# Decays of a gated recurrence from one running sum per 128 tokens, and state products that nobody reads left out

## The chip, the core and the metric

The kernel runs on one core of a Trainium2 chip. The metric is the device time of one launch in microseconds (us), as the median of several runs. The engines of the core are named as in the profile: PE is TensorE (PEld its weight loads), DVE is VectorE, ACT is ScalarE, POOL is GpSimd, SP is SyncE. All five have an instruction queue of their own and work through it in order.

## The reference, cut to what matters

The kernel is an encoder trunk of two layers over 1024 tokens of width 1024: layer 0 mixes tokens by windowed attention, layer 1 by a bidirectional gated linear recurrence, each with a cross attention into 256 memory tokens and each followed by a convolutional feed-forward block. The change lies in the recurrence of layer 1:

```python
def gla_chunked(q, k, v, log_f):          # called once forward, once on flipped time
    b = jnp.cumsum(log_f, axis=2)         # within a chunk
    b_end = b[:, :, -1:]
    q_dec = q * jnp.exp(b)
    k_dec = k * jnp.exp(-b)
    k_end = k * jnp.exp(b_end - b)
    s = jnp.where(causal, q_dec @ k_dec.T, 0)      # inside the chunk
    o_intra = s @ v
    # scan over chunks, per head:
    #   o     = q_dec @ state
    #   state = exp(b_end) * state + k_end.T @ v
```

There are 8 heads with 128 key and 128 value channels. The result does not depend on the size of the chunk, apart from rounding; the state after the last chunk is read by nothing.

## The kernel before

**Staging.** The program is one long stream in which PE has work nearly all the time. The parts follow one another: memory keys and values, layer 0's attention, its output projection, its feed-forward block, then `hgrn()` (layer 1's recurrence, about 1230 to 1910 us of the span), layer 1's output projection and its feed-forward block. Matrix products of weights are done in three products of split operands (`mm3`, lines 79 to 82: high by high, high by low, low by high).

**Order of the instructions.** The source gives a program order; a planner with estimated costs walks through it and sets the order of each engine's queue, taking what it believes to be ready. `tc.high_priority(AHEAD)` lets a group be taken as if it stood 2000 instructions earlier, `tc.issue_after(x)` holds a group until x. Waits for data and for free buffers are put in by the framework: a tile with `bufs=n` has n buffers, and the (n+1)th allocation waits until the readers of the first are done.

**A head.** `proj(h)` makes the projections of head h: q (`sigmoid` on ACT, lines 1091 to 1093, and a product on DVE, line 1129), the two gate inputs `s` (one exponential on ACT, line 1134), and for two heads at a time values and gates (`proj_tm`, lines 1095 to 1115). They land in two PSUM banks `pj`, which ACT and DVE must empty before PE can use them again. `head(h)` then calls `direction` four times, for (forward, tokens 0 to 511), (backward, 512 to 1023), (forward, 512 to 1023) and (backward, 0 to 511), then `output` for both halves. The projections of head h + 1 stand behind it in program order and fill PE while `direction` works on the other engines. `cross` adds the cross attention's pieces in heads 0, 2, 4 and 6; such a head reads its memory keys and values into `kvl` by a DMA, and ACT casts them (line 193).

**`direction`** has keys and channels on the 128 partitions and 512 tokens (four chunks of 128) on the free axis. Four ACT steps make k and the log gate `a_` (lines 1177 to 1180). A scan on DVE sums the log gate, restarted every 16 tokens by `smask`, into `B` (line 1182); `R` is the rest to the end of the 16 (line 1185). ACT makes `EP = exp(B)` and `ER = exp(R)`, and the reciprocals for one half of each pair of 16s (lines 1202, 1203). Four half-size products on DVE give `E1`, `E2`, the operands of the blocks of 32 by 32 tokens on the diagonal. `step(n)` then doubles the reach of EP and ER from n to 2n tokens by two half-size products on DVE (lines 1217, 1218); it is called for 16, 32 and 64. After the first two, `G` for 32 and for 64 is made by one half-size product on POOL (line 1225) and one on DVE (line 1226). 64 small products on PE (`block`, line 1210) fill `pa`, the matrix inside the chunk.

With the reach at 128, EP and ER serve the state: `dec` (POOL, line 1243) takes EP's last column per chunk, `qin` (POOL, line 1245) is EP times q, ER is multiplied by k (DVE, line 1246), turned by four transposes on PE into the bank `pt` (line 1256), copied by ACT to `kT` (line 1258), and multiplied by the values into the bank `pu` (line 1261), four products. The states `S` of the next chunks come from `pu` (lines 1268, 1270). For a chunk without a next one the loop skips the state, but its transpose and its product have been made. `pa` goes through a predicated copy (line 1247) into `Az` and `As`. `output` multiplies `As`, `qin` and `S` into the result, and writes heads 0 to 6 to memory by way of `ot` (line 1315).

A DMA on POOL's queue that sums weights for the feed-forward block in memory (`w2s`) is tied to each `qin` by `sum_steps`.

Of the kernel before, what the change touches and what calls it, by code (L numbers as in the profile page):

```python
# [46 lines left out]
def build(tc, A, out):  # L47
# [983 lines left out]
    def hgrn():  # L1031
# [130 lines left out]
        def direction(h, r, d, b, qin, S, As):  # L1162

            q, k = r["q"][b], r["s"][d][b]
            rev = slice(None, None, -1) if d else slice(None)
            lt, er = (0, 1) if d else (1, 0)

            def E():
                return early.tile([P, 512], F32, tag="E", bufs=5, name="E")
# [6 lines left out]
            a_ = E()  # L1176
            act.activation(k, k, AF.Ln, bias=1.0)
            act.activation(k, k, AF.Exp, scale=-1.0)
            act.activation(a_, k, AF.Ln, bias=lb[:, d, h:h + 1], scale=oml[:, d, h:h + 1])
            act.activation(k, k, AF.Identity, bias=oml[:, d, h:h + 1], scale=noml[:, d, h:h + 1])  # L1180
            R, B = E(), E()
            dve.tensor_tensor_scan(B[:, rev], smask, a_[:, rev], 0.0, op0=ALU.mult, op1=ALU.add)
            v16 = lambda x: x.rearrange("p (b c) -> p b c", c=16)
            e = 0 if d else 15
            dve.tensor_tensor(v16(R), bc(v16(B)[:, :, e:e + 1], [P, 32, 16]), v16(B), op=ALU.subtract)
# [3 lines left out]
            act.activation(EP, B, AF.Exp)  # L1189
            act.activation(ER, R, AF.Exp)  # L1190
            pa = PA[d]
            E1, E2 = E(), E()
            Bl, Be = halves(B, 16)
            Rl, Re = halves(R, 16)
            l1, e1 = halves(E1, 16)
            l2, e2 = halves(E2, 16)

            def parts(n):
                return halves(EP, n) + halves(ER, n) + halves(q, n) + halves(k, n)

            pl_, pe_, rl_, re_, ql, qe, kl, ke = parts(16)
            act.activation(e1, Re, AF.Exp, scale=-1.0)
            act.activation(l2, Bl, AF.Exp, scale=-1.0)
            dve.tensor_tensor(l1, pl_, ql, op=ALU.mult)
            dve.tensor_tensor(e2, re_, ke, op=ALU.mult)
            dve.tensor_tensor(e1, e1, qe, op=ALU.mult)
            dve.tensor_tensor(l2, l2, kl, op=ALU.mult)
            def block(c, i, j, x, y, n=32):

                return pe.matmul(pa[i:i + 32, c, j:j + n], x[:, c * P + i:c * P + i + 32], y[:, c * P + j:c * P + j + n],  # L1210
                                 start=True, stop=True, tile_position=(0, i))

            def step(n):
                pl_, pe_, rl_, re_ = parts(n)[:4]
                e = 0 if d else n - 1
                nb = 512 // (2 * n)
                dve.tensor_tensor(re_, re_, bc(pl_[:, :, e:e + 1], [P, nb, n]), op=ALU.mult)
                dve.tensor_tensor(pl_, pl_, bc(pe_[:, :, e:e + 1], [P, nb, n]), op=ALU.mult)

            for n in (32, 64):  # L1220
                step(n // 2)
                G = E()
                gl, ge = halves(G, n)
                pl_, pe_, rl_, re_, ql, qe, kl, ke = parts(n)
                pool.tensor_tensor(gl, pl_, ql, op=ALU.mult)
                dve.tensor_tensor(ge, re_, ke, op=ALU.mult)
                if n == 32:
                    G32 = G
            with tc.high_priority(AHEAD):
                for c in range(4):  # L1230
                    for o in (0, 32):
                        mm = block(c, er * 64 + o, lt * 64, G, G, 64)
                with tc.issue_after(mm.ins):
                    for c in range(4):
                        for o in range(0, P, 32):
                            block(c, o, o, E2, E1)
                    for c in range(4):
                        for o in (0, 64):
                            block(c, o + er * 32, o + lt * 32, G32, G32)
# [3 lines left out]
            pool.tensor_copy(dec.unsqueeze(2), EP.rearrange("p (c t) -> p c t", t=P)[:, :, e:e + 1])  # L1243
            bs = slice(b * 512, (b + 1) * 512)
            sum_steps[1].send(pool.tensor_tensor(qin[:, bs], EP, q, op=ALU.mult))
            dve.tensor_tensor(ER, ER, k, op=ALU.mult)
            dve.copy_predicated(Az[d], gm[d], pa.rearrange("p c t -> p (c t)"))
            a2 = lambda x: x.rearrange("p c t -> p (c t)")
            if As[b] is None:
                As[b] = wp.tile([P, 4, P], F32, tag="As", bufs=2, name="As")  # L1250
                act.copy(a2(As[b]), Az[d])
            else:
                pool.tensor_tensor(a2(As[b]), a2(As[b]), Az[d], op=ALU.add)
            tp = bank("pt")
            for c in range(4):
                pe.transpose(tp[:, c, :], ER[:, c * P:(c + 1) * P], ident)
            kT = wp.tile([P, 4, P], F32, tag="kT", bufs=1, name="kT")
            act.copy(kT, tp)
            pu = bank("pu")
            for c in range(4):  # L1260
                pe.matmul(pu[:, c, :], kT[:, c, :], r["v"][:, 4 * b + c, :], start=True, stop=True)
            for c in (range(3, -1, -1) if d else range(4)):
                cg = 4 * b + c
                nx = cg - 1 if d else cg + 1
                if not 0 <= nx < NT:
                    continue
                if cg == (NT - 1 if d else 0):
                    act.copy(S[:, nx, :], pu[:, c, :])
                else:
                    dve.scalar_tensor_tensor(S[:, nx, :], S[:, cg, :], dec[:, c:c + 1], pu[:, c, :],  # L1270
                                             op0=ALU.mult, op1=ALU.add)
# [300 lines left out]
```

## Time and profile before

| | us |
|---|---|
| median of 3 runs (lowest to highest) | 2664.08 (2660.1 to 2664.66) |
| time of the profiled execution | 2660.75 |
| its span, first to last instruction | 2658.9 |
| PE busy in it | 2605.2 |
| DVE busy | 1771.2 |
| ACT busy | 1399.1 |
| POOL busy | 472.2 |

The profiled execution is 1.85 us longer than its span, and lies 3.3 us under the median. Busy times are sums over the span; a pipelined matmul counts as busy until its end, so a busy PE isn't PE at its peak. An idle entry behind a row says how long the engine had nothing to do before these instructions, and whose work ended that.

### The profile page before, as it was taken

To read this page: it belongs to the slowest core of one execution; us is meant where nothing else is said; L and a number is where in the kernel's file an instruction comes from. 1 tells how busy PE (TensorE), PEld (TensorE's weight loads), DVE (VectorE), ACT (ScalarE), POOL (GpSimd) and SP (SyncE) were. 2 spreads that over 40 slices of the span, in tenths; PEclk is the share of its full clock that TensorE was granted. 3 is DMA by queue.
4 is the path that set the end of the run, shared out by engine and by line. 5 is a ranking of instruction groups with operands and counts; after the bars stand their busy time and mean duration, and the time that the engine had idled before them with its cause. 6 is when DMAs were issued, how large, how long until landed. Compare 5 with 4: busy or idle time off the path is not lost. (4 is left out here: it accounts for less than half of the span.)

```text
span 2658.9 us, 39054 instructions
## 1 busy us (share of the span) xinstructions
PE 2605.2 (98%) x14420; PEld 2185.9 (82%) x14420; DVE 1771.2 (67%) x2948; ACT 1399.1 (53%) x2534; POOL 472.2 (18%) x520
## 2 busy tenths in 40 slices
PE   8999999999999999999999999999999999999998
PEld 7888887788888888887888878888887788888887
DVE  6678886578555565477677675876757755656447
ACT  6467676545444445455464554656534444445453
POOL 0321010211111100032234131231211111110013
PEclk9999999999999999999999999999999999999999
DMA  9782222367777756674236251103336778785666
GB/s 353 243 176 58 74 86 83 101 193 194 198 201 195 206 154 221 215 265 151 84 112 167 66 124 54 53 25 113 127 105 195 194 193 209 198 202 170 205 207 236
DMA packets 195727, 425.92 MB, mean 160 GB/s; under 512 B 20048, under 2 KB 56272, under 8 KB 189904
## 3 DMA queue, kind: packets, MB, share of 16 engines
q1 hardware_dynamic: 161552, 324.06, 37.6%
q0 software_dynamic: 24544, 90.19, 16.3%
q10 hardware_dynamic: 9440, 9.19, 1.0%
q8 instruction: 113, 1.85, 0.3%
q14 instruction: 78, 0.64, 0.1%
HBM read 330.04 MB, written 116.39 MB: 168 GB/s over the span
## 5 line engine op out<-in xcount | busy, mean ns | idle before, releaser
L86 DVE TENSOR_TENSOR wl<-st,wh 128x1024 fp32r<-128x1024 f32 (+1 forms) x238 | 261.4, 1105 | 316.8 <-ACT wh L85 294.1
L85 ACT CAST wh<-st 128x1024 fp32r<-128x1024 f32 (+1 forms) x238 | 222.4, 937 | 288.7 <-PE X L574 186.5
L80 PE MATMUL pj<-uh,wh 128*128 128x512 f32 x512 | 203.6, 398 | 2.2 <-DVE q L1129 0.8
L574 PE MATMUL X<-wl,wh 128*128 128x512 f32 x528 | 205.0, 390 | 0.3 <-DVE wl L86 0.3
L574 PE MATMUL X<-wh,wl 128*128 128x512 f32 x528 | 204.9, 389 | 0.0
L81 PE MATMUL pj<-ul,wh 128*128 128x512 f32 x512 | 202.4, 395 | 0.0
L82 PE MATMUL pj<-uh,wl 128*128 128x512 f32 x512 | 202.3, 395 | 0.0
L574 PE MATMUL X<-wh 128*128 128x512 f32 x528 | 198.6, 390 | 0.0
L80 PE MATMUL pj<-wh,uh 128*128 128x384 f32 (+1 forms) x512 | 189.4, 372 | 5.0 <-DVE gs L1115 2.6
L82 PE MATMUL pj<-wh,ul 128*128 128x384 f32 (+1 forms) x512 | 187.7, 367 | 0.0
L81 PE MATMUL pj<-wl,uh 128*128 128x384 f32 (+1 forms) x512 | 187.2, 366 | 0.0
L76 DVE TENSOR_TENSOR wl<-st,wh 128x1024 fp32r<-128x1024 f32 (+1 forms) x91 | 113.9, 1256 | 30.9 <-ACT wh L75 29.8
L574 PE MATMUL V<-uh,wh 128*128 128x512 f32 x336 | 130.7, 389 | 0.0
L574 PE MATMUL V<-ul,wh 128*128 128x512 f32 x336 | 130.7, 389 | 0.0
L574 PE MATMUL V<-uh,wl 128*128 128x512 f32 x336 | 130.7, 389 | 0.0
L75 ACT CAST wh<-st 128x1024 fp32r<-128x1024 f32 (+1 forms) x97 | 97.8, 1014 | 37.5 <-PE pj L81 16.4
L574 PEld LDWEIGHTS X<-wl,wh 128*128 128x128 f32 x528 | 99.1, 188 | 21.6 <-DVE wl L86 1.2
L574 PEld LDWEIGHTS X<-wh,wl 128*128 128x128 f32 x528 | 99.1, 188 | 20.7
L574 PEld LDWEIGHTS X<-wh 128*128 128x128 f32 x528 | 99.1, 188 | 20.5
L80 PEld LDWEIGHTS pj<-uh,wh 128*128 128x128 f32 x512 | 96.5, 189 | 21.7 <-DVE q L1129 1.2
L82 PEld LDWEIGHTS pj<-uh,wl 128*128 128x128 f32 x512 | 96.5, 189 | 19.0
L81 PEld LDWEIGHTS pj<-ul,wh 128*128 128x128 f32 x512 | 96.5, 188 | 18.6 <-DVE ul L86 0.4
(411 smaller groups left out, 7149.2 us busy)
## 6 DMA issues: line engine op xcount, KB each, us to landing
st<-hid SPq DMA_DIRECT2D x154, 256.0 KB, 3.4
st<-in_ffw_dram SPq DMA_DIRECT2D x108, 256.0 KB, 3.7
w2s<-in_ffw_dram POOLq DMA_DIRECT2D x24, 1024.0 KB, 8.0
st<-in_ffw_dram SPq DMA_DIRECT2D x46, 512.0 KB, 4.3
hid<-tt SPq DMA_DIRECT2D x88, 256.0 KB, 4.7
st<-w2s SPq DMA_DIRECT2D x88, 256.0 KB, 3.2
sx<-in_ffw_dram SPq DMA_DIRECT2D x84, 256.0 KB, 3.9
sy<-in_ffw_dram SPq DMA_DIRECT2D x42, 512.0 KB, 6.4
```

Of the source, the lines that this page charges most:

```text
L75: act.copy(h[:, :n], raw)
L76: (eng or dve).tensor_tensor(l[:, :n], raw, h[:, :n].bitcast(F32), op=ALU.subtract)
L80: pe.matmul(o, ah, bh, start=first, stop=False)
L81: pe.matmul(o, ah, bl, start=False, stop=False)
L82: return pe.matmul(o, al, bh, start=False, stop=last)
L85: act.copy(h, src)
L86: dve.tensor_tensor(l, src, h.bitcast(F32), op=ALU.subtract)
L574: last = pe.matmul(o, x, y, start=new, stop=e, skip_group_check=not first)
```

## The change

It is all in `hgrn()`. `smask` now restarts the scan every 128 tokens, so B is the sum over a whole chunk. For the reach 16, 32 and 64 a new function subtracts from B its value at the middle of each pair (one full-size subtraction on DVE), and ACT takes exponentials of that difference: two of full size for E1 and E2, two of half size for each G, which the products with q (POOL) and k (DVE) then change in place. `R`, the reciprocals and `step` are gone. EP is the exponential of B itself, ER one exponential per chunk with B's last column as bias, and both are made after the blocks in program order. For the chunk whose state is not read, ER's piece, the transpose and the product are left out, and the copies beside them are shorter. Buffers: tag E has 4 instead of 5, EP and ER 1 each instead of 2, and new tags D (2) and B (1) are added; the sum of buffers is 9 before and after.

```diff
-            gf = early.tile([P, 512], F32, tag="E", bufs=5, name="gf")
+            gf = early.tile([P, 512], F32, tag="E", bufs=4, name="gf")
...
-        pool.memset(smask.rearrange("p (b c) -> p b c", c=16)[:, :, 0:1], 0.0)
+        pool.memset(smask.rearrange("p (b c) -> p b c", c=P)[:, :, 0:1], 0.0)
...
-            R, B = E(), E()
+            B = E("B", 1)
             dve.tensor_tensor_scan(B[:, rev], smask, a_[:, rev], 0.0, op0=ALU.mult, op1=ALU.add)
-            dve.tensor_tensor(v16(R), bc(v16(B)[:, :, e:e + 1], [P, 32, 16]), v16(B), op=ALU.subtract)
-            EP = early.tile([P, 512], F32, tag="EP", bufs=2, name="EP")
-            ER = early.tile([P, 512], F32, tag="ER", bufs=2, name="ER")
-            act.activation(EP, B, AF.Exp)
-            act.activation(ER, R, AF.Exp)
+            def from_middle(n):
+                D = E("D", 2)
+                v = lambda x: x.rearrange("p (b c) -> p b c", c=2 * n)
+                m = n if d else n - 1
+                dve.tensor_tensor(v(D), v(B), bc(v(B)[:, :, m:m + 1], [P, 512 // (2 * n), 2 * n]), op=ALU.subtract)
+                return D
+            D = from_middle(16)
+            E1, E2 = E(), E()
+            act.activation(E1, D, AF.Exp)
+            act.activation(E2, D, AF.Exp, scale=-1.0)
+            dve.tensor_tensor(E1, E1, q, op=ALU.mult)
+            dve.tensor_tensor(E2, E2, k, op=ALU.mult)
...
-            act.activation(e1, Re, AF.Exp, scale=-1.0)
-            act.activation(l2, Bl, AF.Exp, scale=-1.0)
-            dve.tensor_tensor(l1, pl_, ql, op=ALU.mult)
-            dve.tensor_tensor(e2, re_, ke, op=ALU.mult)
-            dve.tensor_tensor(e1, e1, qe, op=ALU.mult)
-            dve.tensor_tensor(l2, l2, kl, op=ALU.mult)
...
             for n in (32, 64):
-                step(n // 2)
-                pool.tensor_tensor(gl, pl_, ql, op=ALU.mult)
-                dve.tensor_tensor(ge, re_, ke, op=ALU.mult)
+                D = from_middle(n)
+                G[n] = E()
+                act.activation(gl, dl, AF.Exp)
+                act.activation(ge, de, AF.Exp, scale=-1.0)
+                pool.tensor_tensor(gl, gl, ql, op=ALU.mult)
+                dve.tensor_tensor(ge, ge, ke, op=ALU.mult)
...
-            step(64)
+            used = [c for c in range(4) if 4 * b + c != (0 if d else NT - 1)]
+            EP, ER = E("EP", 1), E("ER", 1)
+            act.activation(EP, B, AF.Exp)
+            for c in used:
+                x = slice(c * P, (c + 1) * P)
+                m = c * P + (0 if d else P - 1)
+                act.activation(ER[:, x], B[:, x], AF.Exp, bias=B[:, m:m + 1], scale=-1.0)
...
-            dve.tensor_tensor(ER, ER, k, op=ALU.mult)
+            us_ = slice(used[0] * P, (used[-1] + 1) * P)
+            dve.tensor_tensor(ER[:, us_], ER[:, us_], k[:, us_], op=ALU.mult)
...
-            for c in range(4):
+            for c in used:
                 pe.transpose(tp[:, c, :], ER[:, c * P:(c + 1) * P], ident)
...
-            act.copy(kT, tp)
+            act.copy(kT[:, cs_], tp[:, cs_])
...
-            for c in range(4):
+            for c in used:
                 pe.matmul(pu[:, c, :], kT[:, c, :], r["v"][:, 4 * b + c, :], start=True, stop=True)
```

More of the change, by code (lines that the diff above doesn't have):

```diff
@@ L1166, in direction, with E @@
             lt, er = (0, 1) if d else (1, 0)
-            def E():
-                return early.tile([P, 512], F32, tag="E", bufs=5, name="E")
+            def E(tag="E", bufs=4):
+                return early.tile([P, 512], F32, tag=tag, bufs=bufs, name=tag)
             def halves(x, n):
@@ L1211, in block @@
                                  start=True, stop=True, tile_position=(0, i))
[L1213 to L1218, printed above, removed]
-            for n in (32, 64):
-                step(n // 2)
[L1222 to L1225, printed above, removed]
-                dve.tensor_tensor(ge, re_, ke, op=ALU.mult)
-                if n == 32:
-                    G32 = G
+            G = {}
+            for n in (32, 64):
+                D = from_middle(n)
+                G[n] = E()
+                (dl, de), (gl, ge), (ql, _), (_, ke) = (halves(x, n) for x in (D, G[n], q, k))
+                act.activation(gl, dl, AF.Exp)
+                act.activation(ge, de, AF.Exp, scale=-1.0)
+                pool.tensor_tensor(gl, gl, ql, op=ALU.mult)
+                dve.tensor_tensor(ge, ge, ke, op=ALU.mult)
             with tc.high_priority(AHEAD):
@@ L1231, in direction @@
                     for o in (0, 32):
-                        mm = block(c, er * 64 + o, lt * 64, G, G, 64)
+                        mm = block(c, er * 64 + o, lt * 64, G[64], G[64], 64)
                 with tc.issue_after(mm.ins):
@@ L1238, in direction @@
                         for o in (0, 64):
-                            block(c, o + er * 32, o + lt * 32, G32, G32)
-            step(64)
+                            block(c, o + er * 32, o + lt * 32, G[32], G[32])
+            used = [c for c in range(4) if 4 * b + c != (0 if d else NT - 1)]
[5 more added lines that the diff above has]
+                act.activation(ER[:, x], B[:, x], AF.Exp, bias=B[:, m:m + 1], scale=-1.0)
             dec = wp.tile([P, 4], F32, tag="dec", bufs=2, name="dec")
@@ L1254, in direction @@
             tp = bank("pt")
-            for c in range(4):
+            for c in used:
                 pe.transpose(tp[:, c, :], ER[:, c * P:(c + 1) * P], ident)
             kT = wp.tile([P, 4, P], F32, tag="kT", bufs=1, name="kT")
-            act.copy(kT, tp)
+            cs_ = slice(used[0], used[-1] + 1)
+            act.copy(kT[:, cs_], tp[:, cs_])
             pu = bank("pu")
-            for c in range(4):
+            for c in used:
                 pe.matmul(pu[:, c, :], kT[:, c, :], r["v"][:, 4 * b + c, :], start=True, stop=True)
-            for c in (range(3, -1, -1) if d else range(4)):
+            for c in (used[::-1] if d else used):
                 cg = 4 * b + c
                 nx = cg - 1 if d else cg + 1
-                if not 0 <= nx < NT:
-                    continue
                 if cg == (NT - 1 if d else 0):
```

12 lines of the change are left out of this document (1 added, 11 removed).

## The prediction

> **What bounds the kernel now.** I read the page's busy times first, then the recurrence's stretch of the span, then the waits of PE in it, then PE's own order of time around them.
>
> ```profile
> PE 2605.2 (98%) x14420; PEld 2185.9 (82%) x14420; DVE 1771.2 (67%) x2948; ACT 1399.1 (53%) x2534; POOL 472.2 (18%) x520
> ...
> 1230.00:1910.00 680.00, 670.29 (x5280) 564.35 (x5279) 479.67 (x946) 381.30 (x809) 179.60 (x189) 1.00 0.31 90
> ...
> 1380.00:1420.00 40.00, 39.36 (x394) 33.68 (x393) 37.43 (x74) 26.37 (x59) 20.77 (x23) 1.00 0.46 157
> ...
> L1182 DVE TENSOR_TENSOR_SCAN E<-smask,E x3: 1224/1225/1646, 1387.3 to 1411.9; 128x512 f32<-128x512 bf16 x3
> ```
>
> The columns of the stretches are start and end, length, and busy us of PE, PEld, DVE, ACT, POOL, then the granted clock. PE is the bound: 670.3 of 680 us in the only stage that the change touches, at full clock. DVE comes second, and where three directions fall together (the last row: three scans from 1387.3 to 1411.9, 12.3 us apart) it is nearly full itself, 37.4 of 40. So a change gains in two ways only: PE gets less to do, or the 9.7 us for which PE has nothing to do (680 less 670.3) shrink. Those 9.7 us, by what ended them, are these:
>
> ```profile
> PE pj L80 <- DVE gs L1115: 2.6, 3, 1.2
> PE pu L1261 <- DVE S L1270: 2.5, 2, 1.7
> PE pt L1256 <- ACT ot L1315: 2.3, 2, 2.1
> PE pj L80 <- DVE q L1129: 0.8, 1, 0.8
> PE po L1285 <- DVE S L1270: 0.6, 1, 0.6
> PE pt L1296 <- DVE on L1292: 0.4, 1, 0.4
> PE pj L80 <- ACT uh L85: 0.3, 1, 0.3
> ```
>
> Numbers are us in total, times, the longest. 6.9 us wait for DVE (2.6 + 2.5 + 0.8 + 0.6 + 0.4), each a bank that DVE empties late (`gs`, `q`, `S`) or a product that it delivers late (`on`). Only 2.6 us wait for ACT.
>
> **The change part by part. First, PE.** In each head 2 of the 16 pairs of chunk and direction lose their transpose and their product: the last chunk forward, the first chunk backward. Over 8 heads that is 16 transposes and 16 products. What one costs is read from the groups' counts and from starts in PE's order of time, not from durations, since matmuls overlap:
>
> ```profile
> L1261 PE MATMUL pu<-v,kT 128*128 128x128 f32 x256 | 36.7, 276 | 2.5 <-DVE S L1270 2.5
> ...
> L1256 PE MATMUL pt<-ident,ER 128*128 128x128 f32 x128 | 19.6, 280 | 2.3 <-ACT ot L1315 2.3
> ...
> 1871.39 1.05 PE L1261 MATMUL pu<-v,kT 128*128 128x128 f32 x8
> 1872.28 0.60 PE L1256 MATMUL pt<-ident,ER 128*128 128x128 f32 x4
> 1872.63 0.48 PE L80 MATMUL pb<-wh,uh 128*128 128x512 f32 x1
> ```
>
> The source makes 128 of each (8 heads, 4 directions, 4 chunks). The transposes show 128 records, the products 256: each such product is two records. Eight records, four products, take 0.89 us from start to the next start, 0.222 a product; four transposes 0.35, 0.088 each, or, by the length of their row, (0.60 - 0.27) / 3 = 0.11. So 16 x 0.222 = 3.6 and 16 x 0.088 to 0.11 = 1.4 to 1.8: between 5.0 and 5.4 us, and I take 5.1. It lies on PE, the bound, so it comes off the end in full. The small block products stay 64 a direction, and nothing else on PE changes.
>
> **Second, DVE.** The rows of one form each, mean ns:
>
> ```profile
> L1185 DVE TENSOR_TENSOR E<-E 128x512 f32<-128x512 f32 x32 | 21.9, 685 | 1.2
> L1204 DVE TENSOR_TENSOR E<-EP,q 128x256 f32<-128x256 f32 x32 | 18.5, 579 | 0.2 <-ACT EP L1189 0.2
> L1205 DVE TENSOR_TENSOR E<-ER,s 128x256 f32<-128x256 f32 x32 | 20.6, 643 | 7.8 <-ACT ER L1190 7.4
> L1206 DVE TENSOR_TENSOR E<-E,q 128x256 f32<-128x256 f32 x32 | 14.5, 452 | 1.7 <-ACT E L1202 1.7
> L1207 DVE TENSOR_TENSOR E<-E,s 128x256 f32<-128x256 f32 x32 | 13.3, 417 | 0.0
> L1217 DVE TENSOR_TENSOR ER<-ER,EP 128x256 f32<-128x256 f32 x96 | 57.1, 595 | 2.1
> L1218 DVE TENSOR_TENSOR EP<-EP 128x256 f32<-128x256 f32 x96 | 44.2, 460 | 5.8 <-POOL E L1225 1.9
> L1246 DVE TENSOR_TENSOR ER<-ER,s 128x512 f32<-128x512 f32 x32 | 22.8, 714 | 0.1
> ```
>
> Gone: R 21.9, the four half products 18.5 + 20.6 + 14.5 + 13.3, the steps 57.1 + 44.2, in all 190.1 us. New: three full subtractions with a broadcast operand for each of 32 directions, of L1185's form, 96 x 0.685 = 65.8; two full products, 64 x 0.714 (L1246) = 45.7; together 111.5. The scan has the same form and stays. ER's product is a quarter shorter in 16 of 32 directions, 16 x 0.17 = 2.7. Net 81 us less: the stage's 479.7 becomes about 398. This saves nothing by itself, since PE covers it; it acts on the 6.9 us above.
>
> **Third, ACT.**
>
> ```profile
> L1189 ACT ACTIVATE EP<-E 128x512 f32<-128x512 f32 x32 | 20.3, 633 | 56.5 <-DVE E L1182 56.5
> L1202 ACT ACTIVATE E<-E 128x256 f32<-128x256 f32 x32 | 13.0, 407 | 0.0
> L1179 ACT ACTIVATE E<-s,lb,oml 128x512 f32<-128x512 f32 x32 | 26.1, 815 | 2.7 <-DVE oml L1080 1.8
> ```
>
> The exponentials of E1 and E2 take the place of those of EP and ER, two of full size for two. Four of half size for G replace two: 64 more at 0.407 are 26.0 us. EP is one more of full size, 20.3. ER is now 112 pieces of 128 columns (3.5 a direction). No row has that form. Along the two sizes, 0.633 for 512 and 0.407 for 256, a piece of 128 comes to 0.407 - 0.113 = 0.294; the upper end adds what L1179 pays for operands read from a tile, 0.815 - 0.633 = 0.182, so 0.476. L1179 reads two such operands, a piece here one, so I take the middle, 0.385, 43 us (ends 33 and 53). The shorter copy of kT is about 2 us. Net 87 us more, 77 to 97: 381.3 becomes about 468 of 680. In the dense stretch above, with three of the 32 directions in 40 us, ACT goes from 26.4 to about 34.5 and DVE from 37.4 to about 30. POOL keeps its instructions at their sizes, and the `w2s` DMAs stay tied to `qin` on POOL's queue, past which nothing is moved.
>
> **Fourth, the order within a direction.** Before, behind the scan stand R, four half products, two steps and two G products on DVE, one after the other: 0.685 + 2.09 + 2 x (0.595 + 0.460 + 0.44) = 5.8 us until the blocks can start. Afterwards they stand behind one subtraction and six exponentials on ACT, 0.685 + 2 x 0.633 + 4 x 0.407 = 3.6 us, with DVE and POOL beside them, and one product at the end (0.45). Some 1.7 us shorter, 32 times; but PE fills such time with projections, so I cost it at nothing.
>
> **Fifth, buffers and new waits.**
>
> ```profile
>   PE pa L1210: 9.0, 10
> ...
> L1245 POOL TENSOR_TENSOR qin<-EP,q 128x512 f32<-128x512 f32 x32 | 49.2, 1536 | 20.3 <-DVE EP L1218 11.1 <-PE po L1285 9.2
> ...
> POOL dec L1243 <- DVE S L1270: 85.5, 8, 22.3
> ```
>
> The first row stands under the scan, L1182: ten times DVE stood 9.0 us in all because the scan's buffer was still read by the last direction's blocks. B has a buffer of its own now, so this wait goes from DVE. In its place E1's exponential on ACT waits for those blocks (4 uses a direction, 4 buffers), and EP's exponential waits for the last direction's `dec` and `qin` on POOL, one buffer for two; the next scan on DVE waits in turn for EP's and ER's exponentials, which read B. Behind the waiting exponential on ACT stand the evictions of `pj`, and PE waits for these. `qin` takes 1.54 us and `dec` can be held for up to 22.3 us. What speaks against a cost: the planner sees the buffers and puts ACT's evictions ahead of what it believes to be late; directions start some 12 us apart even where they crowd; EP comes last in a direction. Bounds: nothing at one end; at the other, as many waits of the kind for DVE's scan as before, 9.0 us, all of it handed on to PE. I take nothing, as a wait for a scan did not reach PE before either.
>
> **Sixth, the stalls.** How much of PE's 9.7 us stays is open, from none to all. DVE's 6.9 us should fall with DVE's load, 17% less in the stage (81 of 480) and more in the dense stretches where they arise; the evictions through ACT (`gs`, `q`) get a busier ACT instead. I take a third of 6.9, 2.3 us, as gone. The longest stall has its own story:
>
> ```profile
> ACT kvh L193 <- DMA kvl<-kvd: 6.5, 2, 5.9
> ...
> 1538.62 0.39 PE L81 MATMUL pj<-ul,wh 128*128 128x512 f32 x1
> 1538.85 0.39 PE L82 MATMUL pj<-uh,wl 128*128 128x512 f32 x1
> 1541.35 0.66 PE L1256 MATMUL pt<-ident,ER 128*128 128x128 f32 x4 [2.12 <-ACT ot L1315]
> ...
> 1542.00:1544.00 2.00, 1.93 (x7) 0.97 (x5) 0.69 (x1) 1.69 (x4) 0.00 (x0) 0.67 0.35 131
> 1544.00:1546.00 2.00, 1.87 (x7) 1.68 (x8) 0.78 (x2) 2.00 (x5) 0.00 (x0) 0.50 0.35 131
> ```
>
> ACT stood 5.9 us for a DMA, with `ot` behind the cast, and PE stood 2.12 us for `ot`'s bank. The granted clock then fell to 0.67 and 0.50 over two stretches of 2 us: (1 - 0.67) x 2 + (1 - 0.50) x 2 = 1.7 us more. Together 3.8 us for one accident of the order. The Trainium skill (TensorE: Matmul & The Clock Gate, "What's actually happening") lets the clock fall only after an idle window of about 3.4 us; the trace differs, as 2.12 us sufficed, so by the rule this stall would cost 2.1 and by the trace 3.8; if it went, the rule would make 1.7 us less of it. The change does not touch that DMA; new orders on ACT may keep, lose or repeat the accident, so I count it unchanged.
>
> Sum: 5.1 + 2.3 = 7.4 us off the profiled execution's 2660.75, so 2653.4. That execution lies 3.3 us under the median of 2664.08, so against the median the forecast is 2656.7.
>
> **The rivals.** (a) Only PE's 5.1 us go, and the waits for DVE return as waits for a busier ACT, in the same size: 2664.1 - 5.1 = 2659.0. For it speaks that `gs` and `q` each pass three ACT instructions and one on DVE before PE gets its bank; against it that 3.1 of the 6.9 us wait for `S`, which has no ACT step ahead of it except kT's. (b) The stalls go nearly all: DVE was the hidden second bound in the dense stretches, and the accident with the DMA does not fall again. 5.1 + 6.9 + 3.8 = 15.8: 2648.3. For it speaks DVE's 37.4 of 40; against it that the stalls of this order end on seven different pairs of lines, so no one cause holds them. (c) Slower: ACT, in order, stands at EP's exponential for `qin` or `dec`, and `pj` is not emptied. With two banks, PE has about 24 products of 0.23 us (1538.62 to 1538.85 is that pace), 5.5 us, before it stands. It decides from a net cost of 5.3 us on: PE must stand 10.4 us more than now to eat the 5.1 too, which is 1.3 us in each of 8 heads, or three accidents like that of the DMA with the clock's fall. I price it at one such accident in every second head, 4 x 3.8 = 15.2 less 5.1: 2674.2. For it speaks the 22.3 us for which `dec` stood; against it that before, with DVE standing at the scan ten times, PE waited for none of them.
>
> **How the numbers follow.** This kernel's measurement can tell about 0.2%, 5.3 us, from no change. My forecast, 2656.7 with its own range of 2653 to 2660, holds 48%; (a), or stalls that move a few us either way, 27%; (b) 14%; (c) 11%. The bound of 0.2% lies at 2658.75: 42 of the forecast's 48 fall on its faster side, all of (b) and 2 of (a), so faster is 0.58; the other 6, 25 of (a) and 2 of (c) are within 0.2%, 0.33; slower is 0.09. From 2649 to 2665 lie 8 in 10: about half of (b), nearly all of (c) and the ends of (a) are left out.
>
> **What would show it.** The transposes of ER should show 112 records for 128, and the products of `pu` from `kT` 224 for 256; DVE should be busy near 398 and ACT near 468 in a stage some 7 us shorter, and PE's waits for `gs`, `S` and `q` should sum to under 5 us. If EP's exponential shows waits for `qin` or `dec` and PE's waits for ACT grow, (c) is at work; if the waits name ACT at the old total, (a). The prediction would most likely be made wrong by the accidents of order: one stall more over 2 us, with the clock's fall, is worth half of the gain.

## The result, and the profile after

In 22 runs each, beside each other, the changed kernel takes 2669.09 us (2662.42 to 2672.79) and the kernel before 2661.36 us (2658.3 to 2665.32): ratio 1.0025, 95% interval 1.0019 to 1.0032, so 0.25% slower, where 2656.7 and a gain were forecast. The profiled execution took 2670.11 us with a span of 2668.3.

Busy times of the changed kernel's page, the stage, and the dense stretch:

```profile
PE 2606.1 (98%) x14372; PEld 2185.6 (82%) x14372; DVE 1741.2 (65%) x2756; ACT 1456.4 (55%) x2742; POOL 483.3 (18%) x520
...
1230.00:1910.00 680.00, 663.28 (x5189) 556.65 (x5188) 443.75 (x741) 434.71 (x1005) 186.84 (x187) 0.99 0.31 88
...
1380.00:1420.00 40.00, 38.91 (x323) 32.93 (x322) 34.89 (x53) 32.08 (x75) 17.82 (x17) 1.00 0.44 157
...
1230.00:1920.00 690.00, 673.28 (x5241) 565.04 (x5240) 450.47 (x753) 439.82 (x1013) 188.77 (x188) 0.99 0.31 90
```

PE has less work and more busy time: 2606.1 for 2605.2, although by the prediction's sum 5.1 us were taken from it. The recurrence now ends later, so from here on the stretch is 1230 to 1920, in which before looked like this:

```profile
1230.00:1920.00 690.00, 680.29 (x5326) 572.45 (x5325) 485.66 (x956) 385.96 (x818) 181.42 (x191) 1.00 0.32 92
```

PE was idle for 9.7 us of it before (690 less 680.29), and is for 16.7 now. DVE fell by 35 us, not by 81; ACT rose by 54, not by 87. The changed kernel's waits of PE (total, times, longest):

```profile
PE pa L1200 <- DVE E L1211: 4.2, 2, 2.5
PE pj L80 <- DVE gs L1115: 3.5, 3, 1.6
PE pj L80 <- ACT s L1134: 2.5, 4, 1.7
PE pb L80 <- ACT s L1134: 2.2, 1, 2.2
PE pu L1252 <- ACT s L1175: 1.5, 2, 0.8
PE pu L1252 <- DVE S L1259: 1.4, 1, 1.4
PE pu L1252 <- DVE v L1113: 1.1, 1, 1.1
PE pj L80 <- ACT uh L85: 0.3, 1, 0.3
```

The waits for `gs`, `S` and `q`, of which the prediction spoke, did fall, from 6.5 us together to 4.9. What came are new ones: 4.2 us for the blocks, 4.7 for `s` at `pj` and `pb`, 1.5 and 1.1 at `pu`. The first row is the blocks of the recurrence (`pa`), which did not wait once before: they stand for DVE's product that completes G64. Here is its longest wait, in the order of time on ACT, DVE, POOL and PE, and then the clock in stretches of 2 us (third column from the right):

```profile
1457.15 0.41 ACT L1209 ACTIVATE E<-D 128x256 f32<-128x256 f32 x1
...
1457.44 1.22 DVE L1181 TENSOR_TENSOR_SCAN B<-smask,D 128x512 f32<-128x512 bf16 x1
1458.69 1.03 DVE L1188 TENSOR_TENSOR D<-B 128x512 f32<-128x512 f32 x1
1459.65 1.48 DVE L1211 TENSOR_TENSOR E<-E,s 128x256 f32<-128x256 f32 x1
...
1457.54 1.64 POOL L1210 TENSOR_TENSOR E<-E,q 128x256 f32<-128x256 f32 x1
1459.46 1.39 POOL L1234 TENSOR_TENSOR qin<-EP,q 128x512 f32<-128x512 f32 x1 [0.28 <-ACT EP L1225]
...
1461.28 1.89 PE L1200 MATMUL pa<-E 128*32 128x64 f32 x64 [2.46 <-DVE E L1211]
...
1460.00:1462.00 2.00, 0.72 (x17) 0.76 (x21) 2.00 (x4) 0.26 (x1) 2.00 (x3) 0.74 0.94 193
1462.00:1464.00 2.00, 2.00 (x57) 1.84 (x53) 1.65 (x5) 1.57 (x4) 0.61 (x1) 0.50 1.08 225
1464.00:1466.00 2.00, 2.00 (x9) 1.60 (x9) 2.00 (x2) 1.19 (x4) 1.96 (x2) 0.91 1.04 205
```

ACT's exponential is done at 1457.56. The product that needs it starts on DVE 2.1 us later, at 1459.65, because the next direction's scan and first subtraction stand ahead of it in DVE's queue. It then takes 1.48 us beside POOL's `qin`; the median of its row is 0.414 (below). PE, in order, stands 2.46 us, and the clock falls: (0.26 + 0.50 + 0.09) x 2 = 1.7 us more. A wait with a fall of the clock comes three times now (for the blocks 1.76 us at 1272 and 2.46 at 1461, for `s` 2.19 at 1870), once before.

**Where the time went.** Idle time of PE +7.0, the clock's falls 5.1 for 1.7 = +3.4, work -5.1: +5.3 us. The spans differ by 9.4 and the medians by 7.7, so 2 to 4 us are not found in these rows. The clock's part holds for more than the one profiled execution: over all 22 runs the granted clock is 0.9962 in the mean, in the runs of the kernel before beside the experiments 0.9973 to 0.9978, which is 3 to 4 us of 2669.

### The profile page after: what moved, and what is told of

It reads as the page before. It is cut to its first block, busy times and chain, and to the rows that moved or that the text cites. A ratio compares the mean times of both kernels' runs of the same rounds, so it can differ in the third digit from the quotient of the medians.

```text
span 2668.3 us, 38953 instructions
## 1 busy us (share of the span) xinstructions
PE 2606.1 (98%) x14372; PEld 2185.6 (82%) x14372; DVE 1741.2 (65%) x2756; ACT 1456.4 (55%) x2742; POOL 483.3 (18%) x520
## 5 line engine op out<-in xcount | busy, mean ns | idle before, releaser
L962 POOL TENSOR_TENSOR c<-c,g 128x512 f32<-128x512 f32 x24 | 43.4, 1829 | 389.5 <-PE X L574 319.3
```

What stands on the lines that cost most here:

```text
L962: pool.tensor_tensor(y[q][:, t, :], y[q][:, t, :], g3[:, c], op=ALU.mult)
```

## The experiments

All are edits of the kernel before or of the changed one (named), each timed beside the kernel before, whose medians were 2661.4 to 2662.2. The table has, for 1230 to 1920 us of each profile, DVE and ACT busy, PE idle, what the falls of the clock cost (sum of (1 - clock) x 2 us over the stretches under 0.985), and the median time from the start of a scan until G64 is complete, over 32 directions, read from the order of time. G64 is complete when both its halves are, DVE's and POOL's (or the copy, where one was added). In the kernel before POOL's half is the later in all 32 directions, in the changed one in 5. One direction of the kernel before:

```profile
1561.37 0.41 DVE L1226 TENSOR_TENSOR E<-ER,s 128x256 f32<-128x256 f32 x1
...
1561.59 0.79 POOL L1225 TENSOR_TENSOR E<-EP,q 128x256 f32<-128x256 f32 x1 [1.02 <-ACT s L1134]
```

| kernel | us | against before, 95% interval | DVE | ACT | PE idle | clock | scan to G64 |
|---|---|---|---|---|---|---|---|
| before | 2661.4 | | 486 | 386 | 9.7 | 1.7 | 9.3 |
| products_only | 2654.30 | 0.9971 [0.9959, 0.9982] | 483 | 384 | 8.0 | 0 | 9.1 |
| before_ep1 | 2663.94 | 1.0010 [1.0001, 1.0019] | 473 | 383 | 10.4 | 1.7 | 10.5 |
| act_load | 2661.14 | 0.9996 [0.9987, 1.0005] | 476 | 426 | 8.8 | 1.7 | 9.1 |
| before_less_dve | 2656.81 | 0.9974 [0.9963, 0.9985] | 444 | 391 | 5.5 | 0 | 7.0 |
| before_hop | 2658.99 | 0.9983 [0.9974, 0.9992] | 481 | 405 | 6.6 | 0 | 9.6 |
| before_hop2 | 2666.35 | 1.0010 [1.0002, 1.0019] | 501 | 398 | 11.6 | 3.4 | 11.4 |
| after | 2669.09 | 1.0025 [1.0019, 1.0032] | 450 | 440 | 16.7 | 5.1 | 10.5 |
| decays_only | 2678.03 | 1.0058 [1.0046, 1.0071] | 442 | 445 | 19.1 | 13.6 | 10.4 |
| ep_held | 2672.24 | 1.0040 [1.0026, 1.0053] | 441 | 441 | 17.4 | 5.1 | 8.1 |
| g_on_dve | 2669.59 | 1.0030 [1.0018, 1.0041] | 447 | 443 | 17.0 | 6.8 | 10.2 |
| inplace_b2 | 2674.91 | 1.0041 [1.0028, 1.0055] | 456 | 447 | 18.7 | 8.5 | 9.0 |
| k_on_dve | 2678.31 | 1.0062 [1.0050, 1.0075] | 456 | 416 | 21.3 | 11.9 | 10.2 |
| margin | 2671.32 | 1.0036 [1.0023, 1.0050] | 439 | 440 | 18.7 | 6.8 | 8.0 |
| margin_b2 | 2665.47 | 1.0016 [1.0008, 1.0025] | 454 | 447 | 15.4 | 5.1 | 9.4 |
| er_one | 2674.86 | 1.0052 [1.0039, 1.0064] | 450 | 426 | 20.2 | 6.8 | 10.0 |
| no_gq | 2662.84 | 1.0003 [0.9995, 1.0012] | 425 | 446 | 14.6 | 3.4 | 9.3 |
| no_d | 2664.21 | 1.0007 [0.9998, 1.0016] | 420 | 447 | 14.9 | 5.1 | 7.3 |
| no_e_products | 2656.09 | 0.9977 [0.9968, 0.9986] | 423 | 449 | 9.6 | 0 | 8.4 |

The columns from DVE on come from one execution of each kernel, the times are medians of 5 to 22; the execution that no_e_products' columns show took 2660.68, the longest of its 11. Idle and clock together, less 5.1 where the products are left out, give nearly every time: k_on_dve 11.6 + 10.2 - 5.1 = 16.7 for 16.2 measured, no_gq 4.9 + 1.7 - 5.1 = 1.5 for 1.0; the worst are decays_only (21.3 for 16.4) and ep_held (6.0 for 10.6). That shows where the time is, not why. Each edit makes the planner order the stage anew. Four edits that leave the old decays and all products in place (before_ep1, act_load, before_hop, before_hop2) moved by -3.2 to +4.2 us. Six edits of the changed kernel that take no work off DVE (ep_held, g_on_dve, inplace_b2, margin, margin_b2, er_one) lie from 3.6 us below it to 5.8 above it. An effect of that size can hardly be told from that of a new order.

### Which half of the change

products_only is the kernel before with the leave-outs alone; decays_only is the changed kernel with all products made.

```diff
 products_only, against before
+            used = [c for c in range(4) if 4 * b + c != (0 if d else NT - 1)]
-            for c in range(4):
+            for c in used:          # transposes, products; shorter copies
 decays_only, against after
-            used = [c for c in range(4) if 4 * b + c != (0 if d else NT - 1)]
+            used = list(range(4))
```

> The kernel before with only the 16 transposes and 16 state products that nobody reads left out (and the copies beside them shorter); decays as before. Theory 1 (the new decays bring the loss: in the changed kernel the exponentials EP and ER, 1.9 us of ScalarE a direction, are taken ahead of those that the blocks need, so blocks, gate evictions and the clock suffer): nothing of that here, the 5.1 us of TensorE work come off, 2656 against 2661, ratio 0.998, TensorE idle in the recurrence about 9 us as before and at most one fall of the clock. Theory 2 (the plan is redrawn by any edit, and how many stalls over 1.7 us with a fall of the clock it holds is chance): anything from -12 to +6 us; two or three falls of the clock are as likely as one.

> The changed kernel, but with all transposes and state products made again. Theory 1: the loss of the changed kernel plus the 5.1 us of work, about 2674, ratio 1.0045 to the kernel before; TensorE waits for the blocks' operands and for the gate evictions as in the changed kernel. Theory 2: the plan is redrawn, so the stalls are other ones, the total lies anywhere between 2660 and 2676.

Measured: -7.4 us and +16.4 us; their sum, +9.0, is near the +7.7 of both together. products_only has no fall of the clock in the stage, its longest wait is 1.51 us, and it is the fastest kernel of this study. The loss lies in the new decays, and is over twice what the whole change shows. The waits of decays_only, in PE's order of time:

```profile
1270.94 1.92 PE L1200 MATMUL pa<-E 128*32 128x64 f32 x64 [1.76 <-DVE E L1211]
1394.99 0.66 PE L1246 MATMUL pt<-ident,ER 128*128 128x128 f32 x4 [3.04 <-DVE ER L1236]
1560.84 1.12 PE L1246 MATMUL pt<-ident,ER 128*128 128x128 f32 x4 [3.04 <-DVE ER L1236]
1727.37 1.12 PE L1246 MATMUL pt<-ident,ER 128*128 128x128 f32 x4 [3.04 <-DVE ER L1236]
1879.68 0.80 PE L80 MATMUL pb<-wh,uh 128*128 128x512 f32 x1 [4.60 <-ACT s L1134]
```

Five waits, each with a fall of the clock, on three pairs of lines. The first and the last pair, and nearly their moments, are those of the changed kernel; the three waits for ER's product are not there. There is no one wait to take away.

### The order on ACT, and POOL's part of G

In the changed kernel's order of time EP's and ER's exponentials, which nobody needs soon, run ahead of E1's, on which the blocks depend:

```profile
1243.10 0.63 ACT L1225 ACTIVATE EP<-B 128x512 f32<-128x512 f32 x1 [0.51 <-DVE B L1181]
1243.63 1.27 ACT L1229 ACTIVATE ER<-B 128x128 f32<-128x128 f32 x4
1244.81 0.62 ACT L1193 ACTIVATE E<-D 128x512 f32<-128x512 f32 x1
```

ep_held holds them behind the last exponential of G; g_on_dve moves G's product with q from POOL to DVE.

```diff
 ep_held
-            act.activation(EP, B, AF.Exp)
+            with tc.issue_after(last.ins):      # last: exponential of ge
+                act.activation(EP, B, AF.Exp)   # and ER's pieces
 g_on_dve
-                pool.tensor_tensor(gl, gl, ql, op=ALU.mult)
+                dve.tensor_tensor(gl, gl, ql, op=ALU.mult)
```

> The changed kernel with one hold: EP's and ER's exponentials are issued after the last exponential of G. Theory 1: ScalarE reaches the exponentials of E1, E2 and G 1.9 us earlier after the scan, TensorE's waits for VectorE's E (4.2 us) and for ScalarE's s (4.7 us) and two of the three falls of the clock (1.7 us each) go: 6 to 10 us faster than the changed kernel, 2660, ratio 0.997 to 1.000 to the kernel before. Theory 2: the sum of TensorE's idle time stays at 12 to 18 us, with other stalls, and the time within 5 us of the changed kernel. Theory 3 (VectorE's instructions stretched by GpSimd running beside them, 0.68 to 1.8 us, hold up the blocks): no gain beyond 3 us, stretched instructions as often as before.

> The changed kernel with G's product with q on VectorE instead of GpSimd (64 of 0.41 us, 26 us more for VectorE, 71 us less for GpSimd). Theory 3: the new subtractions and products on VectorE, 0.86 to 1.0 us in the mean where an undisturbed one takes 0.68, come down to about 0.75, VectorE's sum in the stage does not rise, the blocks' wait goes, 5 us faster than the changed kernel. Theory 1: the blocks wait for ScalarE's order, so no gain, or a loss of a few us by VectorE's load. Theory 2: within 5 us either way with other stalls.

Measured: 2672.24 and 2669.59, no gain from either. ep_held shortened the way from scan to G64 by 2.4 us (10.5 to 8.1), below the 9.3 of the kernel before, and PE still stood as long, at other moments:

```profile
1546.01 0.69 PE L80 MATMUL pj<-uh,wh 128*128 128x512 f32 x1 [4.38 <-ACT s L1134]
...
1562.99 1.70 PE L1200 MATMUL pa<-E 128*32 128x64 f32 x64 [2.17 <-DVE E L1211]
```

g_on_dve cut its waits at the blocks to 0.8 us, and stood 3.48 and 3.28 us for `s` in their place. Of theory 3's signs two came in part: the subtractions' mean fell from 858 to 810 ns, and DVE's sum did not rise (447 for 450) with 26 us more to do; the gain did not come. That the exponentials run ahead is true, and isn't by itself the cause.

### Single suspects, by themselves

before_ep1 gives the kernel before the changed kernel's single buffers for EP and ER. act_load gives it ACT work that nobody reads: four exponentials of 128 columns a direction. inplace_b2 takes the waits at B away: ER is written over B, which has two buffers. k_on_dve takes 24 us from ACT and gives DVE a row of 20.9.

```diff
 before_ep1
-            EP = early.tile([P, 512], F32, tag="EP", bufs=2, name="EP")   # ER too
+            EP = early.tile([P, 512], F32, tag="EP", bufs=1, name="EP")
 act_load, before R
+            for c in range(4):
+                j = wp.tile([P, P], BF16, tag="junk", bufs=1, name="junk")
+                act.activation(j, B[:, c * P:(c + 1) * P], AF.Exp, bias=oml[:, d, h:h + 1], scale=-1.0)
 inplace_b2, in the changed kernel
-            EP, ER = E("EP", 1), E("ER", 1)
+            EP, ER = E("EP", 1), B     # B: bufs=2; its 4 last columns copied aside on DVE as bias
 k_on_dve, in the changed kernel
-            act.activation(k, k, AF.Identity, bias=oml[:, d, h:h + 1], scale=noml[:, d, h:h + 1])
+            dve.tensor_scalar(k, k, noml[:, d, h:h + 1], oml[:, d, h:h + 1], op0=ALU.mult, op1=ALU.add)
```

> The kernel before with one buffer instead of two for EP and for ER, nothing else. Theory 4 (buffers: in the changed kernel ER's one buffer is held until the transposes have read it, B's one buffer until ER's exponentials have, so the next scan and all behind it start late and the gate evictions on ScalarE stand behind them): the same chain arises here by EP and ER alone, 4 to 12 us slower than the kernel before. Theory 5 (the load of ScalarE, 381 to 437 us in the stage, delays the evictions whatever the buffers): no change beyond 3 us.

> The kernel before with four more exponentials of 128 columns a direction on ScalarE, into a scratch tile that nobody reads, about 50 us of ScalarE in all, as much as the changed kernel adds. Theory 5 (load): TensorE's waits for s, q and gs grow, 6 to 15 us slower than the kernel before, with one or more falls of the clock more. Theory 4 (buffers): within 3 us of the kernel before.

> The changed kernel with ER written in place over B, and the buffer so freed given to B, which now has two (one small copy of the four end columns on VectorE a direction is added, about 5 us). The next scan no longer waits for this direction's ER. Theory 4: the waits of VectorE for ER and of TensorE for s, E and gs shrink, 6 to 12 us faster than the changed kernel, 2657 to 2663, ratio 0.998 to 1.0005 to the kernel before. Theory 5: within 3 us of the changed kernel, 2669, ratio 1.003.

> The changed kernel with the step that turns the gate into k (one full-size ScalarE step a direction, 26 us in all) on VectorE. Theory 5 (load): ScalarE falls by 26 of 437 us, TensorE's waits for s shrink, 4 to 8 us faster than the changed kernel. Theory 4 (buffers): the chain over B and ER is as long, within 3 us of the changed kernel.

Measured: before_ep1 about +2 us, act_load -1, inplace_b2 +12.8 against before (+5.8 against after), k_on_dve +16.2. So single buffers of EP and ER cost the old kernel some 2 us (0.3 to 5 by the interval), and a second buffer for B brought the changed one nothing. 40 us more load on ACT changed nothing in the old kernel; 24 us less of it, paid for on DVE, made the changed one 9 us slower. In k_on_dve ER's product comes late three times, 2.9 us each, so PE's three longest waits are for VectorE.

### Time to spare at the blocks

From the end of G64's later half to the start of the blocks, the kernel before has 0.47 us and more in every direction, the changed one 0.14 or 0.15 in 4 of 32. (The 1.0 us of the expectations counts from DVE's half alone.) margin is ep_held with the blocks held in PE's queue until ER's product is done, so that they come later; margin_b2 is inplace_b2 with both holds.

```diff
 margin, on top of ep_held
+            held = dve.tensor_tensor(ER[:, us_], ER[:, us_], k[:, us_], op=ALU.mult)
+            with tc.issue_after(held.ins):
+                ...                               # the 64 blocks, moved here
```

> The changed kernel with EP's and ER's exponentials held behind the last exponential of G, and the blocks on TensorE held behind ER's product on VectorE, so that the blocks are taken some 2 us after their operands are there, without any more work. Theory 6 (the changed chain crosses from VectorE to ScalarE and back, its end comes 2 us later after the scan than before, the blocks stand in TensorE's queue with no time to spare, and TensorE waits in order): the waits of the blocks for VectorE (4.2 us in the changed kernel, 3.4 with the blocks held nowhere) go to nearly nothing; 3 to 8 us faster than the kernel with the exponentials held alone (2672), 2664 to 2669. Theory 4 (one buffer for B and for ER): the waits for s and gs stay, so no more than that. A rival: the time spared at the blocks comes back at Az, As and the transposes, 2670 or more.

> Both at once: the exponentials EP and ER held, the blocks held behind ER's product, and ER written over B with two buffers of B. If the two causes (no time to spare at the blocks; one buffer for B and ER) are the loss of the new decays, nearly all of it goes: 2654 to 2662, near the kernel with the products alone left out (2654). If the loss lies in the load of VectorE and ScalarE itself, it stays: 2666 or more.

Measured: 2671.32 and 2665.47. In both the blocks still waited for `E` (2.18, 2.16 and 2.90 us): the hold changed the order, and did not make the time to spare that it was to make. So margin does not test its theory; margin_b2 is 3.6 us better than after, within what a new order can do.

### Less work on VectorE, in the changed kernel and in the old one

These leave work out, as their expectations say, so their results are other numbers.

```diff
 no_gq:         - pool.tensor_tensor(gl, gl, ql, op=ALU.mult)
 no_e_products: - dve.tensor_tensor(E1, E1, q, op=ALU.mult)
                - dve.tensor_tensor(E2, E2, k, op=ALU.mult)
 no_d:          -     D = from_middle(n)     # for 32 and 64: D of 16 is used again
 er_one:        -     act.activation(ER[:, x], B[:, x], AF.Exp, bias=..., scale=-1.0)   # 3 or 4 times
                + act.activation(ER, B, AF.Exp)
```

> The changed kernel without the product of G's first half with q on GpSimd (64 instructions, 71 us of GpSimd; this product is left out of the computation). Theory 3 (VectorE's instructions stretched while GpSimd runs): the subtractions D fall from 0.86 us in the mean to under 0.78, VectorE's sum by 15 us or more, and the time by 5 to 10 us to 2659 to 2664. Theory 7 (the chain from the scan to the blocks crosses VectorE and ScalarE in order, with full-size steps): within 3 us of the changed kernel, 2669.

> The changed kernel without the products of E1 with q and E2 with k (64 instructions, 62 us of VectorE; left out of the computation). Theory 7, VectorE's share in it: these stand in VectorE's order between the subtractions for 16 and for 64, so that without them the third subtraction and G's product come 1.7 us earlier; the blocks' wait for VectorE and most of the waits for gs go, 8 to 14 us faster than the changed kernel, 2655 to 2661. If VectorE's share is not the cause: within 3 us of the changed kernel.

> The changed kernel with one full-size exponential for ER instead of 3.5 pieces of 128 columns with a bias (the bias is left out of the computation): 16 us and 80 instructions less of ScalarE, and ER ready 0.6 us earlier. Theory 7, ScalarE's share in it: since EP and ER stand ahead of E1's exponential, the chain is 0.6 us shorter; 2 to 5 us faster than the changed kernel. Theory 3: no change.

> The changed kernel with the subtraction for 16 used for all three levels (64 full-size subtractions on VectorE, about 54 us, are left out, and with them the levels' own middles). G's exponentials then follow E1's and E2's at once, without VectorE between. Theory 7: the handing over between VectorE and ScalarE is the cause, the blocks' wait for VectorE goes and the time falls by 8 to 14 us to 2655 to 2661, more than without the E products if the handing over counts beside the load, equal if only the load of VectorE counts.

Measured against after: -6, -13, +6 and -5 us. no_e_products takes 62 us of DVE's rows away, comes near products_only's time, and shows no fall of the clock in the stage. DVE's sum falls by only 27 us there (450 to 423), since other rows get longer. no_d leaves out two thirds of the subtractions, some 54 us (DVE's sum 420), and gains 5. no_gq takes work from POOL alone, and all that theory 3 expected of it came: the time, DVE's sum (450 to 425, with none of its work left out), and the mean of the subtractions, from 858 to 775 ns:

```profile
L1188 DVE TENSOR_TENSOR D<-B 128x512 f32<-128x512 f32 x96 | 72.5, 775 | 0.6
```

er_one is a plain miss: less ACT work and fewer instructions, and 6 us slower; why is open. Beside it, -6 and -5 are hardly clear of what a new order does; -13 is.

The control for these is the kernel before with as much DVE work left out, and two kernels that lengthen its way to the blocks by copies of G64 in place, without new decays:

```diff
 before_less_dve
-            dve.tensor_tensor(e1, e1, qe, op=ALU.mult)
-            dve.tensor_tensor(l2, l2, kl, op=ALU.mult)
-                step(n // 2)
+                if n == 64: step(n // 2)
 before_hop, before_hop2 (the second line in before_hop2 alone), for n == 64
+                    act.copy(G, G)
+                    dve.tensor_copy(G, G)
```

> The kernel before, without its two in-place half products of E1 and E2 by q and k and without the first of the three steps (n = 16) on VectorE, so its scores are other numbers; 14.5 + 13.3 + 33.8 = 61.6 us of VectorE less, as much as the changed kernel lost when its full products of E1 and E2 were left out (62 us, which gave 13 us back). Chain theory (what the changed kernel loses is its longer chain; the old chain has time to spare): from nothing to 3 us faster than before, 2658 to 2662. VectorE theory (any VectorE time taken from this stage brings PE time, in either kernel): 10 us or more faster, under 2652. Chance of the plan: anywhere within 4 us of before.

> The kernel before with one copy of G64 in place on ScalarE between its products and the blocks: the result is unchanged, the chain from the scan to the blocks is longer by about 1 us (0.63 and two handovers), ScalarE has 20 us more, VectorE nothing more. Chain theory: the blocks' spare time of 1.0 us and up goes, PE shows waits at the blocks for G, and the time is 3 to 8 us over before. VectorE theory: within 2 us of before, as the added ScalarE work of act_load was.

> As before_hop, with one copy more on VectorE behind the one on ScalarE: the chain is longer by about 2 us, as much as the changed kernel's (2.2 us), at 22 us more of VectorE, which then stands at 502 of 680. Chain theory: 8 to 16 us over before, with waits of PE at the blocks of more than 1.7 us and falls of the clock. VectorE theory: 22 us more at the 0.2 us a us that the runs with less VectorE work gave, some 4 us over before, with the waits for gs, S and q rather than at the blocks.

Measured: -5.4, -3.2 and +4.2 us (the last +2.7 by the ratio). before_hop tests the length weakly: as POOL's half was the later one anyway, the way grew by only 0.3 us in the median. But three of its directions have just 0.05 us to spare at the blocks, and it lost nothing. before_hop2 made the way 11.4 us, longer than the changed kernel's 10.5, and lost 4.2 us where 8 to 16 were expected; its waits at the blocks are 0.8 us at most:

```profile
1390.43 1.15 PE L1210 MATMUL pa<-E 128*32 128x64 f32 x64 [0.79 <-DVE E L1229]
...
1557.75 1.15 PE L1210 MATMUL pa<-E 128*32 128x64 f32 x64 [0.79 <-DVE E L1229]
```

Both hops speak against the chain theory in the form in which it stood there. The VectorE theory gave 4 for before_hop2, which was met, and 10 for before_less_dve, which brought half, while the chain theory gave at most 3: that run decides for neither. The same DVE work left out is worth 5.4 us in the old kernel and 13 in the changed one. So the changed kernel is the more sensitive, as far as one order of each can tell; a longer way alone is not the cause.

## Why the prediction was wrong, step by step

**First (PE): right.** The transposes show 112 records and the products 224 (groups of the changed kernel), and products_only gained 7.4 us for the 5.1 worked out, the rest in PE's idle time and the clock.

```profile
L1188 DVE TENSOR_TENSOR D<-B 128x512 f32<-128x512 f32 x96 | 80.3, 858 | 0.5
L1195 DVE TENSOR_TENSOR E<-E,q 128x512 f32<-128x512 f32 x32 | 29.4, 918 | 3.5 <-ACT E L1193 2.8
L1196 DVE TENSOR_TENSOR E<-E,s 128x512 f32<-128x512 f32 x32 | 32.3, 1009 | 0.0
L1229 ACT ACTIVATE ER<-B 128x128 f32<-128x128 f32 x112 | 36.5, 395 | 3.0 <-PE pt L1246 3.0
L1246 PE MATMUL pt<-ident,ER 128*128 128x128 f32 x112 | 18.0, 273 | 0.0
L1252 PE MATMUL pu<-v,kT 128*128 128x128 f32 x224 | 33.1, 276 | 4.0 <-ACT s L1175 1.5 <-DVE S L1259 1.4 <-DVE v L1113 1.1
```

**Second (DVE): a term mis-sized.** The new operations were taken at 0.685 and 0.714 us, 111.5 together; they took 80.3 + 29.4 + 32.3 = 142.0. The two rows that lent their price were hardly disturbed, while rows that were to go were priced at disturbed means (L1217 at 595 ns, with a median of 425). Least, median and longest of a line, in ns, two of the kernel before and three of the changed one:

```profile
L1217 DVE TENSOR_TENSOR ER<-ER,EP x96: 409/425/1291, 1243.9 to 1885.5; 128x256 f32<-128x256 f32 x96
L1246 DVE TENSOR_TENSOR ER<-ER,s x32: 677/684/1656, 1250.6 to 1886.8; 128x512 f32<-128x512 f32 x32
...
L1188 DVE TENSOR_TENSOR D<-B x96: 676/684/1780, 1243.1 to 1899.0; 128x512 f32<-128x512 f32 x96
L1196 DVE TENSOR_TENSOR E<-E,s x32: 669/888/1794, 1246.8 to 1898.4; 128x512 f32<-128x512 f32 x32
L1211 DVE TENSOR_TENSOR E<-E,s x64: 406/414/1515, 1248.5 to 1901.6; 128x256 f32<-128x256 f32 x64
```

Undisturbed they cost what was assumed; some take 2.6 times as long. The order of time shows what stands beside the long ones: of the 96 subtractions the 43 with no POOL instruction beside them took 0.694 us at most, the 53 with one 1.00 in the mean, and with POOL's product away the mean fell (no_gq). So DVE fell by 35 us.

**Third (ACT): price right, weight wrong.** A piece of ER took 0.395 us for the 0.385 taken; the total rose less, as instructions in a row overlap (four pieces in 1.27 us, above). But the step took ACT for the engine to fear, and in act_load, in the old kernel, as much load cost nothing.

**Fourth (order within a direction): failed.** "Some 1.7 us shorter" came out 1.2 us longer (9.32 to 10.53 in the median, 10.25 to 10.68 in the mean; 2.2 in the median to the end of DVE's half alone). The sum, 5.8 and about 4.1 us, counted durations and left out POOL's half and the waits in the queues. The operands now pass from DVE to ACT and back three times, once for each reach, each time behind what stands in the two queues (EP's and ER's exponentials on ACT, the next scan and its subtraction on DVE). By the runs the length as such isn't what costs the time: ep_held went below the old length and gained nothing, before_hop2 exceeded the new one at +4.2.

**Fifth (buffers): about right.** The waits that it named on ACT are there, in place of DVE's 9.0 us at the scan:

```profile
ACT E L1193 <- PE pa L1200: 8.3, 5, 2.6
...
ACT EP L1225 <- POOL dec L1232: 2.2, 2, 1.6
```

After each of the five waits of E1's exponential for the blocks, PE's next wait of over 0.6 us comes 36 us or more later, so they did not reach PE. EP's exponential, rival (c)'s mechanism, stood 2.2 us in all. Single buffers cost some 2 us in before_ep1, and inplace_b2, with two buffers for B, lost 5.8. Rival (c) had the sign, not the place.

**Sixth (stalls): failed, and it is the step that decides.** Of PE's idle time a third of DVE's 6.9 us was to go, and the waits for `gs`, `S` and `q` did fall by 1.6. But new waits, which the fourth and the sixth step put at nothing, came to 11.5 us (blocks 4.2, `s` 4.7, 1.5 and 1.1 at `pu`); the old ones for `ot` and `on`, 2.7, went. So 9.7 us became 16.7, and three waits in place of one set off a fall of the clock. The text named this danger in its last sentence and counted it at nothing in the sum. All eight kernels with the whole of the new decays idle 15 to 21 us, those with the old ones 5.5 to 11.6. So it is not an accident of one order, though which wait it is changes with each edit.

**Shown and open.** Shown: the loss lies in the new decays, not in the leave-outs (+16.4 and -7.4 us alone); it consists of PE's idle time and the clock. No single suspect explains it: not the buffers of EP and ER (some 2 us in the old kernel), not that of B, not the place of EP's and ER's exponentials, not the length of the way alone; and ACT's load was harmless in the old kernel. Leaving out the products of E1 and E2 on VectorE gave 13 us back, which is clear of a new order; the -6 and -5 of no_gq and no_d hardly are. For one wait (at 1461 us) the rows show the cause whole: a product held back 2.1 us by the next direction's work in DVE's queue, and stretched by 1.1 us beside POOL. Argued, not shown: that three passes through the queues of DVE and ACT, with stretched operations ahead, make up the 16 us. One more pass in the old kernel (before_hop2) cost 3 to 4 us, no more than a new order does. What the rest is stays open, as does er_one.

## What to carry to other kernels

Where one engine is 98% busy, leaving out its work that nobody reads paid at once (-7.4 us here), and a change that only relieves other engines is judged by the few longest waits of the bound engine, not by their busy totals. Test the halves of such a change separately: here the good half alone beats the whole by 15 us. Price a new operation with the spread of its kind, and the old ones that it replaces in the same way; then ask what will stand ahead of each step in its queue. When a way between two points is measured, measure it to the last of the operands that its end needs.

## What the runs showed of the hardware

The clock's loss comes in portions: 1.7, 3.4, 5.1, 6.8 us and so on in the table, that is 3.4 us at half clock each. Which wait sets one off isn't told by its length. In no_gq PE waited 1.82 us three times at the same pair of lines (at 1388, 1550 and 1713 us), and the second alone set one off. A wait of 1.75 us with another of 0.79 just ahead of it, at 1272 us, did in margin and did not in ep_held. 2.31 us in no_d (at 1562) and 2.91 in k_on_dve (at 1395) did not; 1.50 with 0.62 close behind did in margin (at 1248). The Trainium skill (TensorE: Matmul & The Clock Gate, "What's actually happening") has a free-running window of about 3.4 us; the portions, and the part that chance plays in whether a wait of 2 to 3 us is hit, agree with it. That a whole idle window is needed does not agree with the waits of 1.75 to 2.5 us that sufficed here.

DVE's operations of 512 columns between 0.67 and 1.79 us in one kernel were the other surprise. The kernel before had the same spread, in rows that the prediction read by their means (L1217 and L1246 above). In the changed kernel all 71 operations of the four new lines (the subtractions and the three products, L1188, L1195, L1196, L1211) that took over 1.3 times the least of their line ran beside a POOL instruction. DVE's product `gs`, which reads a PSUM bank, stayed within 0.390 to 0.426 us, the 8 of 32 beside a POOL instruction included.
